# Low parts of float32 weights made by adding loads, and the lower-bound factor of a gated recurrence moved to its queries: one encoder layer on one core

## The chip, the core and the metric

The kernel runs on one core of a Trainium2 chip. The metric is the device time of one execution in microseconds; three runs of the kernel before took 849.96 to 850.8, with a median of 850.76. The engines are TensorE (PE; its weight loads are PEld), VectorE (DVE), ScalarE (ACT), GpSimd (POOL) and SyncE (SP), which here issues loads.

## The reference, cut to what matters

One layer of a hybrid encoder over 512 tokens of width 1024: token mixing (an attention group beside a bidirectional gated recurrence with 4 heads of 128), cross-attention into 256 memory tokens, and a gated MLP with a short convolution; all in float32. The gates of the recurrence are

```
f = lb_dir + (1.0 - lb_dir) * jax.nn.sigmoid(z)     # one lower bound lb per key column and direction
ks = -jnp.expm1(jnp.log(f))                         # the keys: 1 - f = (1 - lb) * sigmoid(-z)
a = jnp.einsum("...tk,...sk,...tsk->...ts", qx, kx, dec)   # query * key * decay, dec from sums of log f
...
x = x + rmsnorm(mixed, post_mix_g[l])
```

A query and a key meet only in products over the key column k, so a factor that belongs to a column and a direction can stand on either side of that product.

## The kernel before, in words

**Weights.** All weights are packed into 132 units of 128x1024 float32 (512 KB each), in the order of their use: units 0 to 3 are the recurrence's values, 4 to 6 the head 0 (query, forward gate, backward gate), 7 to 10 the output gate, 11 to 16 heads 1 and 2, 17 to 22 the attention's projections, 23 to 25 head 3, 26 to 37 keys and half the values of the memory, 38 to 41 the first half of the output projection; 42 to 131 the rest. Every product is made of three float32r matmuls (`mm3`, L134 to L137): high by high, high by low, low by high. `load_w` (L108) lets SyncE load a unit into one of two `raw` buffers; `issue` (L114) then makes its two parts with `split` (L101): ScalarE casts the unit to float32r (`wh`), and VectorE, for units 28 to 41 GpSimd (`POOL_UNITS`), subtracts that from the unit (`wl`). `wh` and `wl` have 4 buffers each. `unit` (L128) hands a unit to TensorE and issues up to three units ahead of it (`AHEAD`). Units 0 to 3 are split apart from this, by halves (L340 to L366).

**Gated recurrence.** `hgrn_in` (L449) projects a head's queries and its two gates. For each direction, `put_f` makes f and the key from z: two sigmoids on ScalarE (L462, L463), then on VectorE f times (1 - lb) plus lb (L464), the key times (1 - lb) (L465), and q times f into the query of the other direction (L466). `oml` is 1 - lb. `hgrn_core` (L476) then runs a head: the sum of the two keys (L486), its product with q (L489), and nine levels of 1 to 256 tokens, each with a copy of the keys on ScalarE (L496), matmuls (L499), two multiplications by the gates on VectorE (L525), a product of gates (L530) and a masked copy (L531).

**Around them.** `mem_norm` (L629) loads the gains and the two blocks of the memory on GpSimd's queue, squares them on ScalarE (L188), forms the roots on GpSimd (`rstd_of`, L152 to L154) and scales the rows on VectorE (L170). GpSimd has these roots, those of the heads and norms, a product with the output norm's gain (L445) and the loads of gains.

**Order.** Each engine works through its own list in order; the lists come from a scheduler that goes by the program's order and by modelled times of readiness. `weave` (L56) interleaves generators by their given weights: mixing projections beside cores 0 to 2; then core 3, the attention and the memory's projections. Cross-attention and the MLP follow.

Of the kernel before, what the change touches and what calls it, by code (L numbers as in the profile page):

```python
# [9 lines left out]
F32 = mybir.dt.float32  # L10
# [3 lines left out]
ACT = mybir.ActivationFunctionType  # L14
ALU = mybir.AluOpType
# [14 lines left out]
AHEAD = 3  # L30
HOLD_BLOCK = 4
TURN_STEP, MEM_TURN, UP_TURN = 0, (0, 4), (0, 2)
POOL_UNITS = frozenset(range(28, 42))
CORE_SHARE = 53.0
WARM = 4
LEVELS = (1, 2, 4, 8, 16, 32, 64)
# [36 lines left out]
def layer(tc, io, out):  # L73
    nc = tc.nc
# [11 lines left out]
    def small():  # L86
        return sm.tile([P, 16], F32, name="small", tag="small")

    def bank(tag):
        return ps.tile([P, 512], F32, name="ps_" + tag, tag=tag)  # L90

    def big(shape, dt=F32):
        return b8.tile(shape, dt, name="big", tag="big")

    def tmp2(shape=(P, 512), dt=F32, tag="ta"):
        return t2.tile(list(shape), dt, name="tmp2", tag=tag, bufs=TMP_BUFS[tag])
# [4 lines left out]
    def split(hi, lo, src, eng=None):  # L101
        nc.scalar.copy(hi, src)  # L102
        (eng or nc.vector).tensor_sub(lo, src, hi.bitcast(F32))  # L103

    pending, last_pow = deque(), [None]
    issued, taken, last_load = [0], [0], [None]

    def load_w():  # L108
        raw = rawp.tile([P, 1024], F32, name="raw", tag="raw")
        last_load[0] = nc.sync.dma_start(raw, io["w"][issued[0]]).ins  # L110
        issued[0] += 1
        return raw

    def issue():  # L114
        pool_unit = issued[0] in POOL_UNITS
        raw = load_w()
        wh = wp.tile([P, 1024], F32R, name="wh", tag="wh")
        wl = wp.tile([P, 1024], F32R, name="wl", tag="wl")
        split(wh, wl, raw, nc.gpsimd if pool_unit else None)
        pending.append((wh, wl))  # L120

    hold = [N_UNITS]
# [1 line left out]
    def issue_ahead():  # L124
        while issued[0] < min(hold[0], taken[0] + AHEAD):
            issue()

    def unit(n):  # L128
        taken[0] += 1
        issue_ahead()  # L130
        wh, wl = pending.popleft()
        return wh.rearrange("p (k n) -> p k n", k=n), wl.rearrange("p (k n) -> p k n", k=n)
# [6 lines left out]
    def blk(b):  # L139
        return slice(b * P, (b + 1) * P)  # L140
# [96 lines left out]
    def proj_fm(act, n, tag, use):  # L237
        o = bank(tag)
        w = unit(8)
        for kc in range(8):  # L240
            mm3(o[:, :n], (w[0][:, kc, :], w[1][:, kc, :]), act.get(kc, slice(0, n)), kc == 0, kc == 7)
            if kc % 2 and kc < 7:
                yield 6 * MM * n / 512
        use(o)
        yield 6 * MM * n / 512
# [57 lines left out]
    nhalf = const.tile([P, 16], F32, name="nhalf")  # L303
# [3 lines left out]
    nc.gpsimd.memset(ones, 1.0)  # L307
    nc.vector.memset(warm[:, :256], 0.0)
    nc.gpsimd.memset(nhalf, -0.5)

    def load_xt(kc, n):
        nc.sync.dma_start(xt[kc // 4][:, kc % 4:kc % 4 + n, :], io["xt"][:, kc:kc + n, :])

    raw = rawp.tile([P, 1024], F32, name="raw", tag="raw")
# [38 lines left out]
    for j in range(4):  # L353
        if j >= 2:
            w_raw.append(load_w())
        wh = wp.tile([P, 1024], F32R, name="wh", tag="wh")
        wl = wp.tile([P, 1024], F32R, name="wl", tag="wl")
# [15 lines left out]
    for _ in range(2):  # L373
        issue()
# [35 lines left out]
    lb = const.tile([P, 2, 4], F32, name="lb")  # L410
    oml = const.tile([P, 2, 4], F32, name="oml")
# [20 lines left out]
    def scaled(put):  # L432
        def use(o):
            z = tmp2()
            nc.vector.tensor_mul(z, o, r_bc)
            put(z)
        return use
# [11 lines left out]
    def hgrn_in(h, between=(), raw=False):  # L449
        qk = big([P, 2, 2, T])  # L450
        tt = big([P, 2048])
        q = tmp2(tag="tq")

        def put_q(z):
            nc.scalar.activation(q, z, ACT.Sigmoid)
            nc.vector.tensor_mul(q, z, q)

        def put_f(d):
            def put(z):
                f = tt[:, d * T:(d + 1) * T]  # L460
                k = qk[:, 1, d, :]
                nc.scalar.activation(f, z, ACT.Sigmoid)  # L462
                nc.scalar.activation(k, z, ACT.Sigmoid, scale=-1.0)  # L463
                nc.vector.tensor_scalar(f, f, oml[:, d, h:h + 1], lb[:, d, h:h + 1], op0=ALU.mult, op1=ALU.add)  # L464
                nc.vector.tensor_scalar(k, k, oml[:, d, h:h + 1], None, op0=ALU.mult)  # L465
                nc.vector.tensor_mul(qk[:, 0, 1 - d, :], q, f)  # L466
            return put

        for put in (put_q, put_f(0), put_f(1)):
            yield from proj_fm(raw_act if raw else hT, T, "b", scaled(put) if raw else put)  # L470
            for job in between[:2]:
                job()
            between = between[2:]
        heads[h] = (q, qk, tt)

    def hgrn_core(h):  # L476
        while h not in heads:
            yield None
        q, qk, tt = heads[h]
# [3 lines left out]
        st = room[:, 1536:1792].rearrange("p (g n) -> p g n", g=2)  # L483
        diag = a[:, :, 0, :]
        ksum = tmp2(tag="th")
        nc.vector.tensor_add(ksum, qk[:, 1, 0, :], qk[:, 1, 1, :])  # L486
        o = bank("c").rearrange("p (b n) -> p b n", b=NB)
        for b in range(NB):
            nc.tensor.matmul(o[:, b, :], ksum[:, blk(b)], q[:, blk(b)], start=True, stop=True)  # L489
# [58 lines left out]
        for b in range(NB):  # L548
            nc.vector.scalar_tensor_tensor(out=on[:, b, :], in0=o[:, b, :], scalar=r[:, b:b + 1],
                                           in1=sg_box[0][:, b, blk(h)], op0=ALU.mult, op1=ALU.mult)  # L550
# [104 lines left out]
    def cores():  # L655
        for h in range(3):
            yield from hgrn_core(h)
# [95 lines left out]
    def attention_filler():  # L753
# [7 lines left out]
        kv["y0"] = yield from res_first(mix, MIX_ORDER, lambda j: rec_done[0] == 4 if j >= 2 else att_done[0] >= 2 * j + 2)  # L761

    weave((hgrn_core(3), 22.0), (attention(), 42.0), (attention_filler(), 52.0))

    x = load_x()
# [126 lines left out]
    for kc in range(NF):  # L892
# [3 lines left out]
        w = unit(1)  # L896
# [110 lines left out]
```

## Time and profile before

| | |
|---|---|
| median of 3 runs | 850.76 us (849.96 to 850.8) |
| profiled execution, its own time | 851.05 us |
| its span, first to last instruction | 849.3 us, so 1.75 us lie around it |
| mean granted TensorE clock | 0.996 |
| busy TensorE, VectorE, ScalarE, GpSimd | 828.8, 526.6, 401.1, 95.9 us |
| loads issued by SyncE | 131 units of 512 KB and others, 77.44 MB on its queue |

Times in views of the profile are microseconds from the first instruction, unless marked ns. A row of a group gives line, engine, operation, what it writes and reads, the shape and the count, then the busy time and the mean of one, then the idle time of the engine before them. A matmul's end is modelled, so that matmuls overlap in the records; the distance from one start to the next is the pace. Times of GpSimd are rough. The chain is followed back from the last instruction to what released each step.

### The profile page before, as it was taken

The numbers are of one execution on the slowest core, as the hardware profiler recorded it, in microseconds if no ns is written. First come the engines' busy times: TensorE is split into PE (matmuls) and PEld (weight loads), VectorE is DVE, ScalarE is ACT, GpSimd is POOL, SyncE is SP. The second block draws the span as 40 slices with busy tenths as digits, with TensorE's granted clock in tenths as the row PEclk, the third lists the DMA queues.
The fourth block names the chain that finished last, engine by engine and source line by source line (L and its number), as shares of the span: only waits on it lengthen the run. The fifth ranks groups of instructions, "written<-read, shape, count | busy, mean of one in ns | idle before, by whom it ended". The sixth has DMA issues, their size and how long they took to land.

```text
span 849.3 us, 11048 instructions
## 1 busy us (share of the span) xinstructions
PE 828.8 (98%) x4304; PEld 702.9 (83%) x4304; DVE 526.6 (62%) x799; ACT 401.1 (47%) x710; POOL 95.9 (11%) x128
## 2 busy tenths in 40 slices
PE   8979999999999999999999999999999999999996
PEld 6868888887889888888888998888888888888885
DVE  5598497969997774854443865555555557722224
ACT  6563345445878884644543643333333335511121
POOL 0311100224243301300001300000000000000001
PEclk9999999999999999999999999999999999999999
DMA  9722202122222224252312242223233332322212
GB/s 323 232 76 75 74 25 87 51 76 75 75 75 91 78 81 175 75 174 75 100 50 75 76 135 98 95 94 100 100 100 99 100 100 79 101 96 97 100 49 100
DMA packets 24756, 83.52 MB, mean 98 GB/s; under 512 B 3264, under 2 KB 3904, under 8 KB 24704
## 3 DMA queue, kind: packets, MB, share of 16 engines
q1 hardware_dynamic: 22752, 77.44, 27.5%
q0 software_dynamic: 1232, 4.46, 1.7%
q10 hardware_dynamic: 720, 0.92, 0.3%
q8 instruction: 34, 0.56, 0.3%
q14 instruction: 18, 0.15, 0.1%
HBM read 80.71 MB, written 2.10 MB: 98 GB/s over the span
## 4 chain that ended last, share of the span: by engine, by line
PE 87%; DVE 6%; DMA 3%; ACT 2%; issue 1%; POOL 0%; POOLq 0%; DVEq 0%; ACTq 0%
PE ps_b L135 9%; PE ps_b L136 9%; PE ps_b L137 9%; PE ps_s L137 6%; PE ps_s L135 6%; PE ps_s L136 6%; PE ps_o L135 6%; PE ps_o L137 6%; PE ps_o L136 6%; PE ps_c L135 4%; PE ps_c L136 4%; PE ps_c L137 4%; PE ps_c L499 3%; DMA raw<-in_w_dram 2%; PE ps_o L717 2%; DVE big L525 1%
## 5 line engine op out<-in xcount | busy, mean ns | idle before, releaser
L103 DVE TENSOR_TENSOR wl<-raw,wh 128x1024 fp32r<-128x1024 f32 x114 | 139.4, 1223 | 219.7 <-ACT wh L102 219.6
L102 ACT CAST wh<-raw 128x1024 fp32r<-128x1024 f32 x128 | 134.6, 1052 | 243.5 <-PE ps_o L137 80.5
L135 PE MATMUL ps_b<-big,wh 128*128 128x512 f32 (+1 forms) x320 | 118.0, 369 | 0.0
L136 PE MATMUL ps_b<-big,wh 128*128 128x512 f32 (+1 forms) x320 | 116.6, 364 | 0.0
L137 PE MATMUL ps_b<-big,wl 128*128 128x512 f32 (+1 forms) x320 | 116.5, 364 | 0.0
L137 PEld LDWEIGHTS ps_b<-big,wl 128*128 128x128 f32 x320 | 60.3, 188 | 9.3
L135 PEld LDWEIGHTS ps_b<-big,wh 128*128 128x128 f32 x320 | 60.4, 189 | 9.1
L136 PEld LDWEIGHTS ps_b<-big,wh 128*128 128x128 f32 x320 | 60.4, 189 | 8.9
L163 POOL TENSOR_SCALAR small<-small 128x1 f32<-128x1 f32 x40 | 14.0, 350 | 440.6 <-ACT tmp L194 421.7
L135 PE MATMUL ps_s<-wh,big 128*128 128x512 f32 (+1 forms) x140 | 53.8, 384 | 0.0
L137 PE MATMUL ps_s<-wh,big 128*128 128x512 f32 (+1 forms) x140 | 53.4, 382 | 0.0
L136 PE MATMUL ps_s<-wl,big 128*128 128x512 f32 (+1 forms) x140 | 52.9, 378 | 0.0
L525 DVE TENSOR_TENSOR big<-big 128x512 f32<-128x512 f32 x64 | 49.8, 786 | 2.7 <-PE ps_c L499 1.6
L135 PE MATMUL ps_o<-wh,big 128*128 128x512 f32 (+1 forms) x124 | 47.5, 383 | 0.0
L137 PE MATMUL ps_o<-wh,big 128*128 128x512 f32 (+1 forms) x124 | 47.3, 381 | 0.0
L136 PE MATMUL ps_o<-wl,big 128*128 128x512 f32 (+1 forms) x124 | 47.1, 380 | 0.0
L103 DVE TENSOR_TENSOR big<-ps_o,big 128x512 fp32r<-128x512 f32 x52 | 35.8, 688 | 15.9 <-ACT big L102 15.5
L103 POOL TENSOR_TENSOR wl<-raw,wh 128x1024 fp32r<-128x1024 f32 x14 | 33.9, 2424 | 57.9 <-ACT wh L102 49.2
L102 ACT CAST big<-ps_o 128x512 fp32r<-128x512 f32 x52 | 30.4, 585 | 19.9 <-PE ps_o L814 7.5
L135 PE MATMUL ps_b<-wh,big 128*128 128x512 f32 x92 | 36.6, 398 | 0.0
L136 PE MATMUL ps_b<-wl,big 128*128 128x512 f32 x92 | 36.1, 392 | 0.0
L137 PE MATMUL ps_b<-wh,big 128*128 128x512 f32 x92 | 36.0, 391 | 0.0
(246 smaller groups left out, 1891.7 us busy)
## 6 DMA issues: line engine op xcount, KB each, us to landing
raw<-in_w_dram SPq DMA_DIRECT2D x131, 512.0 KB, 3.3
big<-in_x_dram SPq DMA_DIRECT2D x8, 512.0 KB, 7.3
big<-in_xt_dram SPq DMA_DIRECT2D x3, 512.0 KB, 8.0
big<-in_mem_dram POOLq DMA_DIRECT2D x2, 512.0 KB, 9.4
out_dram<-big SPq DMA_DIRECT2D x4, 256.0 KB, 2.1
out_dram<-big ACTq DMA_DIRECT2D x3, 256.0 KB, 2.1
big<-in_xt_dram SPq DMA_DIRECT2D x2, 256.0 KB, 3.4
raw<-in_w_dram SPq DMA_DIRECT2D x2, 256.0 KB, 4.0
```

Of the source, the lines that this page charges most:

```text
L102: nc.scalar.copy(hi, src)
L103: (eng or nc.vector).tensor_sub(lo, src, hi.bitcast(F32))
L135: nc.tensor.matmul(o, a[0], b[0], start=start, stop=False)
L136: nc.tensor.matmul(o, a[0], b[1], start=False, stop=False)
L137: nc.tensor.matmul(o, a[1], b[0], start=False, stop=stop)
L163: nc.gpsimd.tensor_scalar(ss[:, i + 4:i + 5], ss[:, i:i + 1], 1.0 / D, ss[:, i + 3:i + 4] if i else EPS, op0=ALU.mult, op1=ALU.add)
L499: nc.tensor.matmul(o[:, b, :], kc[:, blk(b)], pat(qk, b * P, [[2 * m, P // (2 * m)], [T + m, 2], [1, m]]), start=True, stop=True)
L525: nc.vector.tensor_tensor(out=c, in0=c, in1=pat(tt, toff + off, [[2, npair], [gap, 2], [0, m]]), op=ALU.mult)
L717: nc.tensor.matmul(o, vv[:, c, h // 4].rearrange("p a d -> p (a d)"), pt[:, j, c, :], start=c + j == 0, stop=c == 3 and j == 1)
```

## The change

`issue` makes the low part of units 4 to 41 in another way. After the cast to `wh`, `wl` is set to minus `wh`, by ScalarE for units 4 to 27 and by GpSimd for units 28 to 41, and a load issued by GpSimd reads the unit from memory a second time and adds it to `wl`. In `put_f`, f is made by ScalarE (Identity with scale and bias), the key stays without its factor (1 - lb), and the factor goes into the product of q and f. The keys' sum in `hgrn_core` takes the factors itself: half of it on ScalarE, the other half and the sum on VectorE. At the start, ScalarE copies a small tile.

```
-POOL_UNITS = frozenset(range(28, 42))
+NEG_SCALAR = frozenset(range(4, 28))
+NEG_POOL = frozenset(range(28, 42))
...
     def issue():
-        pool_unit = issued[0] in POOL_UNITS
+        i = issued[0]
         raw = load_w()
         wh = wp.tile([P, 1024], F32R, name="wh", tag="wh")
         wl = wp.tile([P, 1024], F32R, name="wl", tag="wl")
-        split(wh, wl, raw, nc.gpsimd if pool_unit else None)
+        if i in NEG_SCALAR or i in NEG_POOL:
+            nc.scalar.copy(wh, raw)
+            if i in NEG_SCALAR:
+                nc.scalar.mul(wl, wh.bitcast(F32), -1.0)
+            else:
+                nc.gpsimd.tensor_scalar(wl, wh.bitcast(F32), -1.0, 0.0, op0=ALU.mult, op1=ALU.add)
+            nc.gpsimd.dma_start(wl, io["w"][i], accum_op=ALU.add)
+        else:
+            split(wh, wl, raw)
         pending.append((wh, wl))
...
     nc.gpsimd.memset(nhalf, -0.5)
+    nc.scalar.copy(small(), nhalf)
...
-                nc.vector.tensor_scalar(f, f, oml[:, d, h:h + 1], lb[:, d, h:h + 1], op0=ALU.mult, op1=ALU.add)
-                nc.vector.tensor_scalar(k, k, oml[:, d, h:h + 1], None, op0=ALU.mult)
-                nc.vector.tensor_mul(qk[:, 0, 1 - d, :], q, f)
+                nc.scalar.activation(f, f, ACT.Identity, scale=oml[:, d, h:h + 1], bias=lb[:, d, h:h + 1])
+                nc.vector.scalar_tensor_tensor(out=qk[:, 0, 1 - d, :], in0=f, scalar=oml[:, d, h:h + 1], in1=q,
+                                               op0=ALU.mult, op1=ALU.mult)
...
-        nc.vector.tensor_add(ksum, qk[:, 1, 0, :], qk[:, 1, 1, :])
+        nc.scalar.mul(ksum, qk[:, 1, 0, :], oml[:, 0, h:h + 1])
+        nc.vector.scalar_tensor_tensor(out=ksum, in0=qk[:, 1, 1, :], scalar=oml[:, 1, h:h + 1], in1=ksum,
+                                       op0=ALU.mult, op1=ALU.add)
```

## Rows read from the trace of the kernel before

**Rows 1.** The page, busy us, share of the span and instructions of each engine.

```profile
PE 828.8 (98%) x4304; PEld 702.9 (83%) x4304; DVE 526.6 (62%) x799; ACT 401.1 (47%) x710; POOL 95.9 (11%) x128
```

**Rows 2.** Stretches: length, then busy us (count) of PE, PEld, DVE, ACT, POOL; clock, DMA share, GB/s.

```profile
0.00:20.00 20.00, 17.37 (x61) 13.68 (x62) 10.82 (x18) 12.46 (x20) 0.44 (x6) 1.00 0.90 320
...
40.00:60.00 20.00, 15.56 (x69) 12.57 (x67) 16.27 (x25) 13.81 (x20) 3.17 (x4) 1.00 0.27 86
60.00:80.00 20.00, 18.83 (x108) 16.34 (x108) 18.87 (x33) 6.27 (x9) 0.00 (x0) 0.91 0.15 52
...
140.00:160.00 20.00, 19.68 (x151) 18.45 (x150) 19.55 (x42) 9.70 (x20) 2.15 (x4) 1.00 0.17 53
...
200.00:220.00 20.00, 17.36 (x113) 15.39 (x112) 18.21 (x28) 12.69 (x22) 7.20 (x4) 1.00 0.18 59
220.00:240.00 20.00, 19.37 (x150) 17.86 (x149) 19.42 (x42) 17.14 (x36) 8.21 (x4) 1.00 0.23 80
240.00:260.00 20.00, 18.56 (x147) 17.37 (x146) 18.05 (x32) 15.16 (x32) 6.78 (x4) 1.00 0.24 80
...
640.00:660.00 20.00, 20.00 (x90) 16.58 (x89) 10.37 (x12) 8.18 (x10) 0.00 (x0) 1.00 0.25 84
```

**Rows 3.** TensorE's waits: line waited for, us in total, times, longest us.

```profile
PE ps_c L489 <- DVE tmp L486: 6.7, 2, 5.6
```

**Rows 4.** Chain that ended last, 54 to 62 us: start us, us, what.

```profile
54.50 1.05 ACT tmp L188 x2
...
60.51 0.61 DVE tmp L486
```

**Rows 5.** Chain that ended last, 200 to 216 us: start us, us, what.

```profile
202.43 2.23 DVE big L464
...
210.78 1.85 DVE big L464
...
214.89 1.16 PE ps_c L489 x8
```

**Rows 6.** VectorE's groups by form: busy us, mean ns, idle before.

```profile
L103 DVE TENSOR_TENSOR wl<-raw,wh 128x1024 fp32r<-128x1024 f32 x114 | 139.4, 1223 | 219.7 <-ACT wh L102 219.6
...
L464 DVE TENSOR_SCALAR big<-big,oml,lb 128x512 f32<-128x512 f32 x8 | 7.4, 926 | 0.3 <-ACT big L462 0.3
...
L465 DVE TENSOR_SCALAR big<-big,oml 128x512 f32<-128x512 f32 x8 | 3.8, 478 | 0.0
```

**Rows 7.** GpSimd's groups by form.

```profile
L103 POOL TENSOR_TENSOR wl<-raw,wh 128x1024 fp32r<-128x1024 f32 x14 | 33.9, 2424 | 57.9 <-ACT wh L102 49.2 <-PE ps_s L695 5.2 <-DMA raw<-in_w_dram 3.4
...
L634 POOL DMA_DIRECT2D big<-in_mem_dram x2 | 1.1, 540 | 0.0
L409 POOL CAST masks<-tmp 128x896 uint8<-128x896 f32 x1 | 0.9, 929 | 1.7 <-DMA tmp<-in_masks_dram 1.7
```

**Rows 8.** ScalarE's groups by form.

```profile
L102 ACT CAST wh<-raw 128x1024 fp32r<-128x1024 f32 x128 | 134.6, 1052 | 243.5 <-PE ps_o L137 80.5 <-PE ps_b L136 69.5 <-PE ps_c L136 33.4
...
L681 ACT ACTIVATE tmp<-tmp,small 128x512 f32<-128x512 f32 x22 | 15.8, 725 | 4.6 <-DVE small L677 4.5
...
L335 ACT ACT_TABLE_LOAD x1 | 1.3, 1283 | 3.8 <-DMA big<-in_xt_dram 3.8
```

**Rows 9.** Loads by line: queue, count, KB each, median us from issue to landing.

```profile
raw<-in_w_dram SPq DMA_DIRECT2D x131, 512.0 KB, 3.3
...
big<-in_mem_dram POOLq DMA_DIRECT2D x2, 512.0 KB, 9.4
...
big<-in_mem_norm_g_dram POOLq DMA_DIRECT2D x1, 512.0 KB, 7.9
...
big<-in_post_x_g_dram POOLq DMA_DIRECT2D x1, 512.0 KB, 4.3
```

**Rows 10.** Timelines of ScalarE and TensorE, 22 to 32 us: start us, us, what.

```profile
22.39 1.03 ACT L102 CAST wh<-raw 128x1024 fp32r<-128x1024 f32 x1
...
31.12 0.39 PE L137 MATMUL ps_b<-big,wl 128*128 128x512 f32 x1
```


## The prediction, made before the changed kernel was run

> **What bounds the kernel now.** The busy line of the page comes first: TensorE is busy for 98% of the span, VectorE for 62%, ScalarE for 47%, GpSimd for 11% [rows 1]. A change to the three vector engines can therefore only pay where TensorE waits for them, so the second view is the table of 20 us stretches [rows 2]. From about 340 us on, every stretch looks like 640:660: TensorE 20.00 of 20, 90 matmuls, one each 222 ns. That part is fixed, and no unit touched by the change lies in it. What can move is idle time before it: 4.44 us in 40:60 and 1.17 in 60:80, which belong to one wait; 0.32 in 140:160; and 2.64, 0.63 and 1.44, together 4.71, in 200:260. VectorE has 18 to 19.4 of 20 us taken in those last three stretches and 19.55 in 140:160.
>
> The third view is the list of TensorE's waits: the longest, 5.6 us, is that of L489, the first matmul of core 0, for the keys' sum of L486 [rows 3]. The fourth, the chain that ended last, says why: before L486 (60.51) stand the two squares of the memory rows on ScalarE (from 54.50), GpSimd's two roots, then the scaling L170 on VectorE [rows 4]. The wait also costs after it: the granted clock of 60:80 is 0.91, that is 9% of 20 us or some 1.8 us at less than 2.4 GHz, behind a TensorE that had done nothing. In 200:216 the chain is VectorE's: L464, the gates' multiply-and-add, stands in it with 2.23 and 1.85 us, and core 3's L489 (214.89) follows [rows 5]. The mean of L464 is 926 ns against 478 for the like L465 [rows 6]; the long ones fall together with GpSimd's 2.42 us subtractions [rows 7], so one of the two engines holds the other up.
>
> **The change, part by part.** Units 4 to 27 lose a VectorE subtraction of 1.22 us each, 29.3 us in all, and gain a ScalarE multiplication of the same 128x1024, priced by the cast of that size at 1.05 us [rows 6, 8], plus a GpSimd-issued load of the unit's 512 KB that adds onto the tile. Units 28 to 41 change GpSimd's 2.42 us subtraction for a one-input multiply-add. Its price is not shown; the nearest are the cast of 896 elements at 0.93 us below and the subtraction above, and I take 1.1 by the cast, which has one input as well. Issuing a load costs GpSimd 0.54 us [rows 7].
>
> The adding load itself is nowhere in the trace. Below it is a plain 512 KB load, 3.3 us; GpSimd's own took 4.3 in a calm stretch (the gains of the second norm) and 7.9 near the start beside other loads (those of the memory's) [rows 9]. Above I put 12.7, the 9.4 of the memory rows and 3.3 for a second pass over the bytes (an estimate from these rows). I take 7.9 at the start and 4.3 later. A unit lasts 24 matmuls of 222 ns, 5.3 us, and is prepared three units ahead, 16 us. Cast, multiplication, issue and load make 1.05 + 1.05 + 0.54 + 4.3 = 6.9 us, and 15.3 at the upper end: behind the start both fit, though the latter with hardly 1 us to spare. The 38 second reads, 19.9 MB over some 300 us, add about 66 GB/s to stretches with 52 to 86, where 0:20 moved 320: hidden.
>
> (a) *Unit 4.* Its cast runs at 22.39 and TensorE's first matmul on the low part at 31.12 [rows 10]. Now 22.39 + 1.03 + 1.05 + 0.54 + 7.9 = 32.9: TensorE waits 1.8 us (0 with 4.3, 6.6 with 12.7; more if GpSimd first does the scaled identities L382 that it is busy with then). TensorE comes 1.8 us later to a wait of 5.6, so this is nothing at the end so long as L489 is let go no later than that wait allows: the cover is that wait. If (b) removed it, the 1.8 would count.
>
> (b) *The wait of L489.* VectorE loses in 40:60 four subtractions and two pairs L464/L465, but the chain there runs over ScalarE's squares. ScalarE had 13.81 of 20 us taken; it gets four multiplications (4.2), two gates' Identity and half the sum, each like the scaled copy L681 at 0.73 [rows 8]: 6.4 more, and is full. In order, what stands before the squares holds them up, and GpSimd's roots, the scaling and the sum after them. Three multiplications and two Identities all in front would be 4.6 later; with the squares ahead of the gates the sum could start some 3.9 earlier (gates' last sigmoid at 54.5, then 0.73 + 0.73 + 0.75). Nearest is that its idle time takes most of it: I take +1.0. Queued behind GpSimd's new issues are its roots; a load that waits for a late multiplication holds those too, inside the same bounds.
>
> (c) *60 to 200 us.* ScalarE has room (6.3 to 9.7 of 20), VectorE loses some 1.2 us a unit. The idle shown is 0.32 in 140:160, with VectorE all but full. Shorter waits don't show where a matmul's modelled end reaches over the next one's start (the row of 31.12 lasts 0.39 us, and 0.22 is the pace); 0.08 us of them at each of the 14 levels of cores 1 and 2 is my estimate, with the 0.32 some -1.5. Bounds: -3, and +2.1, where two multiplications stand in front of a level's key copy.
>
> (d) *200 to 260 us.* Both L464 leave the chain, 2.23 and 1.85 us, and two L465 of 0.48; the product with q stays. Less one Identity each, 0.73, on ScalarE, that is some 3.6 us off the way to 214.89, more than the 2.64 idle of 200:220; I close that, and 0.9 of the 2.07 behind, as GpSimd's holds shrink from 2.4 to 1.1: -3.5. Next late there are the casts and Identities on ScalarE. Bounds -4.7 and 0.
>
> (e) *The small copy at the start* may bring the 1.28 us table load [rows 8] ahead of the first tile. TensorE would then only come sooner to (a)'s wait: 0, at best -1.3, and 0 if a copy needs no table.
>
> Sum: 1.0 - 1.5 - 3.5 = **-4.0 us** on this execution's 851.05 (span 849.3, 1.75 around it), that is 847.05; it stands 0.29 above the median of the runs, 850.76. Forecast **847 us**.
>
> A rule of the Trainium skill speaks against the loads: the page SBUF — State Buffer, Who interferes with whom, says that GpSimd and VectorE lock each other out of a shared pair of ports, and that descriptors which GpSimd writes for a load starve meanwhile (620 ns became about 3100). L464's 2.23 us above agrees with the lock; no run here shows the starving. By it unit 4's low part would be up to 2.5 us later, the wait 4.3 and not 1.8, and the sum -1.5 if 2.5 of it were not covered.
>
> **Rivals.** *Late low parts at the start (ends slower, 0.27).* If the adding load takes much longer than a plain one, TensorE, which waited nowhere between 31.1 and 55.6 (61.17 less 5.6), waits at unit 4 for 6.6 us and loses clock as it did in 60:80, 1.8 more; the memory rows' load and roots stand behind these issues on GpSimd, so the cover at L489 slips with it. 6.6 + 1.8 + 1.0 - 5.0 = +4.4: 855 us. It decides from about 5 us of uncovered wait, where the later gains are used up; loads near 10 us do that. For it: beside other loads they took 7.9 and 9.4, about twice the calm 4.3 [rows 9]. Against: the 7.9 is one of those.
>
> *Relief spent elsewhere (same, 0.13).* ScalarE, 15 to 17 of 20 in 220:260, or the full ScalarE of (b) becomes what TensorE waits for; (b) at +3 and (d) at -1.5, with (c) at -1.5, leave 850.8. For: the gates now take three ScalarE steps. Against: units 28 to 41 put nothing more on ScalarE.
>
> *The wait at L489 shrinks as well (faster, 0.10).* With (b) at -3.9, its clock loss of 1.8 gone and (e) at -1.3, beside (c) and (d): 851.05 - 0.29 - 12.0, about 839. For: VectorE is relieved just there. Against: the squares.
>
> The forecast itself, 842 to 849.5, has 0.50. I set what a measurement of this kernel can tell from no change at 0.2%, 1.7 us. **Range 838 to 856**: it leaves out loads slower than the bound and all gains together. Faster 0.58 (forecast and last rival, less their edge), same 0.14, slower 0.28, the rivals' own with 0.01 of that edge each.
>
> **What would show it.** Right: no VectorE wl subtraction for units 4 to 41; L464 gone and core 3's wait for the keys' sum (214.89) under 0.5 us; a wait of 0 to 3 us near 31 us, for a DMA; L489 near 62 us with a shorter wait before it; 200:260 with TensorE idle near 1.2 us. Wrong: TensorE waits for wl after 60 us, landings over 10 us, a clock row under 1.00 near 30 us, ScalarE as releaser of the keys' copy, or idle in 200:260 unchanged.

## The result, and the profile of the changed kernel

The changed kernel takes **852.34 us** (median of 6 runs, 851.94 to 854.2) against 850.51 (6 runs, 847.26 to 851.27) for the kernel before: a ratio of 1.0027, with a 95% interval of 1.0014 to 1.004. It is slower, by 1.8 us between the medians, where 847 and faster was forecast; the time lies inside the range of 838 to 856. The profiled execution took 851.94 us, its span is 850.2.

The busy line of the page does not show it: VectorE has 38 us less to do than in [rows 1], ScalarE and GpSimd have 31 and 12.5 more, and TensorE is busy for 98% of the span as before.

```profile
PE 829.1 (98%) x4304; PEld 703.2 (83%) x4304; DVE 488.9 (58%) x759; ACT 431.8 (51%) x747; POOL 108.4 (13%) x166
```

The table of stretches does, read against [rows 2] (columns as there: stretch, length, busy us and count of PE, PEld, DVE, ACT, POOL, then clock, DMA share, GB/s):

```profile
0.00:20.00 20.00, 18.41 (x72) 14.62 (x73) 10.94 (x18) 12.97 (x21) 0.45 (x6) 1.00 0.89 325
20.00:40.00 20.00, 13.68 (x55) 10.93 (x54) 4.87 (x12) 15.29 (x24) 8.06 (x11) 0.83 0.89 241
40.00:60.00 20.00, 20.00 (x90) 16.52 (x88) 12.21 (x19) 13.95 (x21) 3.39 (x5) 1.00 0.78 211
60.00:80.00 20.00, 15.98 (x89) 13.46 (x87) 16.08 (x29) 11.45 (x16) 4.20 (x7) 0.91 0.66 159
...
140.00:160.00 20.00, 19.37 (x155) 18.66 (x154) 16.91 (x39) 13.54 (x26) 4.66 (x8) 1.00 0.58 129
...
200.00:220.00 20.00, 20.00 (x126) 17.20 (x124) 15.79 (x30) 15.39 (x27) 6.73 (x8) 1.00 0.72 162
220.00:240.00 20.00, 18.98 (x144) 17.68 (x144) 18.94 (x34) 16.39 (x33) 6.19 (x6) 1.00 0.69 153
240.00:260.00 20.00, 19.66 (x157) 18.64 (x157) 17.53 (x36) 16.88 (x36) 6.55 (x7) 1.00 0.77 162
```

TensorE idles 6.32 us in 20:40, where it was never idle before; nothing in 40:60 rather than 4.44; 4.02 in 60:80 rather than 1.17. In 200:260 it idles 0 + 1.02 + 0.34 = 1.36 us rather than 4.71. So the late stage gave what was forecast, and the first 80 us, where the clock fell as well (0.83 in 20:40), took more than that. The list of TensorE's waits names the three places (columns as in [rows 3]):

```profile
PE ps_b L146 <- DMA wl<-in_w_dram: 6.3, 1, 6.3
PE ps_c L501 <- DVE tmp L497: 3.0, 1, 3.0
PE ps_c L511 <- DVE big L537: 2.0, 3, 1.0
```

The first is unit 4's low part; the second is core 0's wait for the keys' sum, 5.6 us in [rows 3]; of the third, the longest, 1.0 us at core 0's second level (69.00), is new. The chain from 24 to 70 us shows what stands before each (start us, us, what):

```profile
24.12 2.32 POOL tmp L392 x4
26.45 8.64 DMA wl<-in_w_dram
35.13 0.79 PE ps_b L146
35.92 0.43 PE ps_b L144
...
53.64 0.57 POOL wl L126
54.21 10.02 DMA big<-in_mem_dram
...
66.43 1.42 DVE big L179 x2
67.84 1.03 DVE big L537
69.00 1.20 PE ps_c L511 x8
```

Unit 4's adding load stands behind GpSimd's four scaled identities (L392), is issued at 26.45 and takes 8.64 us to land. After that wait the matmuls pace at 0.43 us, against 222 ns in the calm stretches. Two stretches cut around the wait show the clock: 0.81 us of TensorE's work in 28:35, and behind it a granted clock of 0.50, the 1.2 GHz level, for 4 us, which costs about half of them, 2 us.

```profile
28.00:35.00 7.00, 0.81 (x5) 0.37 (x4) 1.70 (x3) 3.50 (x5) 2.61 (x3) 0.83 1.01 267
35.00:39.00 4.00, 3.87 (x9) 3.10 (x10) 1.88 (x3) 4.00 (x7) 0.00 (x0) 0.50 1.06 277
```

The second half of the chain is the memory rows. Before, the gains' and both rows' loads (L148, L634) stood right behind the masks' cast in GpSimd's queue, and GpSimd made the roots from 55.6 us. Now five adding loads (L126) stand ahead of the first and a sixth ahead of the second, each waiting for ScalarE's multiplication (L123). GpSimd's timeline:

```profile
48.42 0.86 POOL L126 DMA_DIRECT2D wl<-in_w_dram  x1 [8.46 <-ACT wl L123]
48.97 0.87 POOL L157 DMA_DIRECT2D big<-in_mem_norm_g_dram  x1
49.54 0.86 POOL L646 DMA_DIRECT2D big<-in_mem_dram  x1
53.64 0.88 POOL L126 DMA_DIRECT2D wl<-in_w_dram  x1 [3.24 <-ACT wl L123]
54.21 0.85 POOL L646 DMA_DIRECT2D big<-in_mem_dram  x1
```

VectorE then meets the scaling of those rows (L179) ahead of the keys' sum (L497) and again ahead of a pair product (L537) of the first level:

```profile
60.90 1.41 DVE L179 SCALAR_TENSOR_TENSOR big<-big,small 128x512 f32<-128x512 f32 x2 [3.48 <-ACT wl L123]
62.57 0.75 DVE L497 SCALAR_TENSOR_TENSOR tmp<-big,oml,tmp 128x512 f32<-128x512 f32 x1
```

### The profile page after: what moved, and what is told of

Its sections match the earlier page's. It is cut to its first block, busy times and chain, and to the rows that moved or that the text cites. A ratio compares the mean times of both kernels' runs of the same rounds, so it can differ in the third digit from the quotient of the medians.

```text
span 850.2 us, 11098 instructions
## 1 busy us (share of the span) xinstructions
PE 829.1 (98%) x4304; PEld 703.2 (83%) x4304; DVE 488.9 (58%) x759; ACT 431.8 (51%) x747; POOL 108.4 (13%) x166
## 4 chain that ended last, share of the span: by engine, by line
PE 87%; DMA 4%; DVE 4%; ACT 3%; issue 1%; POOL 1%; SPq 0%; POOLq 0%; DVEq 0%; ACTq 0%
PE ps_b L146 9%; PE ps_b L145 9%; PE ps_b L144 9%; PE ps_s L146 6%; PE ps_s L145 6%; PE ps_s L144 6%; PE ps_o L144 6%; PE ps_o L145 6%; PE ps_o L146 6%; PE ps_c L145 4%; PE ps_c L146 4%; PE ps_c L144 4%; PE ps_c L511 3%; PE ps_o L729 2%; DMA raw<-in_w_dram 1%; DVE big L537 1%
## 5 line engine op out<-in xcount | busy, mean ns | idle before, releaser
L104 DVE TENSOR_TENSOR wl<-raw,wh 128x1024 fp32r<-128x1024 f32 x90 | 110.2, 1224 | 199.5 <-ACT wh L103 199.4
L121 ACT CAST wh<-raw 128x1024 fp32r<-128x1024 f32 x38 | 39.9, 1049 | 30.7 <-PE ps_b L145 13.4
L537 DVE TENSOR_TENSOR big<-big 128x512 f32<-128x512 f32 x64 | 49.3, 777 | 8.1 <-PE ps_c L511 3.5
L126 POOL DMA_DIRECT2D wl<-in_w_dram x38 | 34.1, 897 | 107.3 <-ACT wl L123 82.1
L144 PE MATMUL ps_b<-wh,big 128*128 128x512 f32 x92 | 36.6, 398 | 0.0
```

Of the source, the lines that this page charges most:

```text
L121: nc.scalar.copy(wh, raw)
L126: nc.gpsimd.dma_start(wl, io["w"][i], accum_op=ALU.add)
L144: nc.tensor.matmul(o, a[0], b[0], start=start, stop=False)
L537: nc.vector.tensor_tensor(out=c, in0=c, in1=pat(tt, toff + off, [[2, npair], [gap, 2], [0, m]]), op=ALU.mult)
```

## The experiments

Each time is a median, given beside that of the kernel before from runs on the same chip in between; the ratio of the runs (not quite that of the medians) and its 95% interval follow. From set to set the kernel before moved between 850.36 and 850.87, so times of different sets compare to about 0.5 us. "A" is the theory that the loss sits at the start (unit 4's late low part and the memory rows queued behind adding loads).

Two things bear on all of them. First, the busy rows understate what TensorE loses, since a matmul's modelled end reaches over the next one's start. The table counts the 4304 matmuls of each profiled execution by their starts instead, at their middle distances (0.227 us for 512 columns, 0.120 for 256, 0.111 for 128), and gives how far TensorE falls behind that pace in each stretch, in us. It is an estimate; its sums differ as the spans do, to 0.4 us. In the first column, executions of like lists differ by up to 1.8 (experiments 3, 11 and 12).

| kernel | 0:80 | 80:200 | 200:260 | 260:340 |
|---|---|---|---|---|
| before | 15.2 | 4.4 | 6.6 | 1.0 |
| changed | 20.0 | 4.2 | 3.0 | 1.0 |
| 1, new gates, no loads | 12.6 | 3.3 | 11.1 | 1.1 |
| 2, loads, old gates | 19.4 | 3.8 | 1.0 | 1.0 |
| 3, copy alone | 12.8 | 4.3 | 6.6 | 1.0 |
| 4, from unit 10, new gates | 13.5 | 3.9 | 3.3 | 1.0 |
| 5, from unit 28, new gates | 13.6 | 3.3 | 3.4 | 1.0 |
| 6, from unit 10, old gates | 12.4 | 3.6 | 1.2 | 1.0 |
| 11, from unit 28, old gates | 14.2 | 4.3 | 1.6 | 1.0 |
| 12, as 11 without loads | 14.6 | 4.5 | 1.6 | 1.0 |
| 13, all on ScalarE, new gates | 13.4 | 4.0 | 2.4 | 2.9 |
| 14, all on ScalarE, old gates | 12.1 | 3.6 | 2.5 | 2.4 |

Second, the scheduler makes every version's lists anew, and an edit can move steps that it does not name. TensorE's order is that of the kernel before in 3, 11 and 12, that of the changed kernel in 8, 9 and 10, and another in the rest. On VectorE the scaling of the memory rows stands ahead of core 0's keys' sum in the kernel before and in 3, 7, 11 and 12 (both blocks) and in the changed kernel and 8, 9 and 10 (one block); in 1, 2, 4, 5, 6, 13 and 14 it stands behind. What those experiments say of the first 80 us holds for edit and list together.

**1. New gates and copy, no adding loads.**

```diff
-NEG_SCALAR = frozenset(range(4, 28))
-NEG_POOL = frozenset(range(28, 42))
+NEG_SCALAR = frozenset()
+NEG_POOL = frozenset()
+POOL_UNITS = frozenset(range(28, 42))
...
-            split(wh, wl, raw)
+            split(wh, wl, raw, nc.gpsimd if i in POOL_UNITS else None)
```

> The new gates, the new keys' sum and the small copy stay; all low parts of weights are formed as in the kernel before (VectorE, GpSimd for units 28 to 41). Theory A (the loss sits at the start: unit 4's low part, 6.5 us of wait and some 2 of half clock, and the memory rows that queue behind the adding loads): 845 to 848 us, since the 3.4 us of idle closed in 200:260 stay and the start is that of before or a little earlier. Theory B (the three ScalarE steps of the gates cost what the loads gave): 850 or more. The first matmul on unit 4's low part waits for nothing under both.

Measured: **852.71** against 850.59, 1.0016 (1.0008 to 1.0025). A's number failed and B's was met; B's reason is weighed at 13 and 14. The start is as A had it: 73.45 of the first 80 us busy, against 71.77 in the kernel before and 68.06 in the changed one. But 200:260 got worse, with 7.30 us idle (60 − 52.70) and a lower clock:

```profile
200.00:260.00 60.00, 52.70 (x384) 47.91 (x383) 53.30 (x91) 43.73 (x84) 18.44 (x9) 0.97 0.22 71
```

So taking L464 away does not close that stage. The timelines of VectorE and GpSimd show what stands there now: a pair product (L538) meets GpSimd's subtraction (L105) and takes 3.35 us; the one before it, with GpSimd idle, took 1.15. Others beside that step took 2.9 and 2.55, and L601 2.78 rather than 0.68; VectorE's reductions from PSUM (L686) kept 0.67 to 0.69 beside it.

```profile
215.93 1.15 DVE L538 TENSOR_TENSOR big<-big 128x512 f32<-128x512 f32 x1 [0.28 <-ACT tmp L509]
217.57 3.35 DVE L538 TENSOR_TENSOR big<-big 128x512 f32<-128x512 f32 x1 [0.50 <-PE ps_c L512]
```

```profile
217.53 2.39 POOL L105 TENSOR_TENSOR wl<-raw,wh 128x1024 fp32r<-128x1024 f32 x1 [6.79 <-PE ps_c L512]
```

**2. Adding loads alone**, with the old gates and sum and without the copy.

```diff
-    nc.scalar.copy(small(), nhalf)
...
-                nc.scalar.activation(f, f, ACT.Identity, scale=oml[:, d, h:h + 1], bias=lb[:, d, h:h + 1])
-                nc.vector.scalar_tensor_tensor(out=qk[:, 0, 1 - d, :], in0=f, scalar=oml[:, d, h:h + 1], in1=q,
-                                               op0=ALU.mult, op1=ALU.mult)
+                nc.vector.tensor_scalar(f, f, oml[:, d, h:h + 1], lb[:, d, h:h + 1], op0=ALU.mult, op1=ALU.add)
+                nc.vector.tensor_scalar(k, k, oml[:, d, h:h + 1], None, op0=ALU.mult)
+                nc.vector.tensor_mul(qk[:, 0, 1 - d, :], q, f)
...
-        nc.scalar.mul(ksum, qk[:, 1, 0, :], oml[:, 0, h:h + 1])
-        nc.vector.scalar_tensor_tensor(out=ksum, in0=qk[:, 1, 1, :], scalar=oml[:, 1, h:h + 1], in1=ksum,
-                                       op0=ALU.mult, op1=ALU.add)
+        nc.vector.tensor_add(ksum, qk[:, 1, 0, :], qk[:, 1, 1, :])
```

> The adding loads for units 4 to 41 alone, on the kernel before (old gates, old sum, no small copy). Theory A: 854 to 857 us: unit 4's wait of 4 to 6.5 us with a clock row under 1.00 behind it, the wait for the keys' sum not shorter than 3 us, and nothing given back in 200:260 but what GpSimd's shorter step gives to L464 (0 to 2). Theory B: 849 to 851, as the loads relieve VectorE.

Measured: **849.0** against 850.59, 0.9977 (0.9968 to 0.9987); A's number failed, B's was met at its lower edge, and it is faster than the whole change. The start costs what A had (19.4 against 15.2 in the table; unit 4 waits 3.7 us), but the loads alone close 200:260 to 0.33 us of idle, more than they do beside the new gates (1.36):

```profile
200.00:260.00 60.00, 59.67 (x441) 55.38 (x440) 53.13 (x107) 48.39 (x92) 20.89 (x21) 1.00 0.75 167
```

**3. The small copy alone** (all else of the kernel before).

```diff
+    nc.scalar.copy(small(), nhalf)
```

> The small copy at the start alone, on the kernel before. Theory A: the first v matmul comes about 1 us earlier, and the wait for core 0's keys' sum (5.6 us before) grows by as much, since the memory rows do not come earlier: 850 to 851 us. Theory C (what is won at the start stays to the end): 848.5 to 849.5.

Measured: 850.2 against 850.59, 0.9995 (0.9983 to 1.0007): not to be told from no change. The timelines show what it does: the table load runs at 1.17 us rather than at 3.81, and the first v matmul starts at 5.17 rather than 6.38. The profiled execution, at 848.67 the second fastest of 11 (848.34 to 851.18), keeps its gain to the end: 2.4 us less lost by 80 us in the table, and the same behind. The median shows 0.4; what takes the gain in the other executions no trace shows. A's reason does not appear: the wait for the keys' sum is 5.1 us and has not grown.

**4. Adding loads from unit 10 on**; units 4 to 9 keep VectorE's subtraction.

```diff
-NEG_SCALAR = frozenset(range(4, 28))
+NEG_SCALAR = frozenset(range(10, 28))
```

> The changed kernel, but units 4 to 9 keep VectorE's subtraction; adding loads begin with unit 10, so that none stands ahead of the memory rows in GpSimd's queue. Theory A: 843 to 848 us, no wait for a load of wl before 60 us, the memory rows' loads issued near 30 us as before, 200:260 with 1.4 us idle. Theory D (adding loads cost wherever they are, by the engines that serve the loads): 850 or more, with PE idle or short waits in 80:200 where the 32 loads are.

Measured: **845.51** against 850.59, 0.9929 (0.9916 to 0.9941). A holds, D falls: the 32 loads that are left cost nothing that shows (3.9 us lost in 80:200, against 4.3 in experiment 3). With the first six the changed kernel is 6.8 us slower than this one. The idle of 200:260 is 1.37, as in the changed kernel.

```profile
200.00:260.00 60.00, 58.63 (x434) 54.15 (x434) 51.49 (x100) 50.02 (x98) 18.55 (x19) 1.00 0.72 160
```

The rows' loads are issued at 31.09 and 31.63, but no row stands ahead of the sum any more: VectorE's list has the scaling behind it.

```profile
53.89 0.75 DVE L497 SCALAR_TENSOR_TENSOR tmp<-big,oml,tmp 128x512 f32<-128x512 f32 x1 [1.26 <-ACT big L473]
...
56.69 1.42 DVE L179 SCALAR_TENSOR_TENSOR big<-big,small 128x512 f32<-128x512 f32 x2 [0.74 <-POOL small L163]
```

**5. Adding loads for units 28 to 41 alone**, new gates and copy.

```diff
-NEG_SCALAR = frozenset(range(4, 28))
+NEG_SCALAR = frozenset()
```

> New gates, sum and copy, and adding loads for units 28 to 41 alone; units 4 to 27 are split by VectorE. Theory E (the idle of 200:260 hangs on GpSimd's 2.4 us subtractions, which stretch whatever VectorE does beside them; L464 was only one victim): against 852.7 us of the run with the gates and no loads, some 6 less: 845.5 to 848, with TensorE idle under 2.5 us in 200:260 and VectorE's pair products there back from 1.23 us to 0.9 or less. Theory F (what closes 200:260 is that VectorE is rid of the splits of units 4 to 27 before): 851 to 853 with the idle of 7.3 still there.

Measured: **845.18** against 850.63, 0.9928 (0.9916 to 0.9941). E holds, 0.3 us under its range: with the splits of units 4 to 27 back on VectorE, the idle of 200:260 is 60 − 58.31 = 1.69 us, against 7.30 in experiment 1. What closes that stage is GpSimd's step.

```profile
200.00:260.00 60.00, 58.31 (x438) 53.98 (x437) 52.89 (x103) 50.49 (x99) 18.23 (x19) 1.00 0.72 159
```

**6. As 4, with the old gates and sum** (edit of 4, and that of 2 without its first line).

> Adding loads from unit 10 to 41 and the small copy, with the gates and the keys' sum of the kernel before. Theory E with the gates as a cost of their own (1.0 us of idle in 200:260, wait for ScalarE's Identity): 843 to 845 us, under the 845.5 of the same with the new gates; idle under 0.6 us in 200:260. Theory G (the new gates gain once the loads have freed ScalarE's rival, VectorE): 847 or more.

Measured: **842.38** against 850.63, 0.9901 (0.9887 to 0.9914): the fastest here, 0.6 us under E's range, 8.25 us under the kernel before and 10 under the changed one. The idle of 200:260 is 0.32.

```profile
200.00:260.00 60.00, 59.68 (x451) 55.94 (x450) 51.74 (x107) 50.23 (x98) 19.05 (x19) 1.00 0.75 168
```

**7. Memory rows' loads ahead in the queue.**

```diff
+    kv = {}
+    kv["g"], = gains("mem_norm_g")
+    kv["rows"] = big([P, MB, D])
+    for b in range(MB):
+        nc.gpsimd.dma_start(kv["rows"][:, b, :], io["mem"][blk(b), :])
     def normalize(kc):
...
     def mem_norm():
-        g_mem, = gains("mem_norm_g")
-        kv["rows"] = big([P, MB, D])
+        g_mem = kv["g"]
         for b in range(MB):
             m = kv["rows"][:, b, :]
-            nc.gpsimd.dma_start(m, io["mem"][blk(b), :])
```

> The changed kernel, but the loads of the memory's rows and gains are put ahead, behind unit 5's adding load in GpSimd's queue rather than behind unit 9's. If the memory rows' lateness is the half of the start's loss that is not unit 4's: unit 4's wait of about 6.3 us stays, the waits of 3.0 for the keys' sum and 1.0 at core 0's first level go, 847.5 to 849.5 us. If the sum is held by ScalarE's steps for the gates: 851.5 to 853.

Measured: **847.54** against 850.63, 0.9963 (0.9949 to 0.9977). The loads are issued from 28.8 us; unit 4's wait stays (5.3), the wait for the sum all but goes (0.6), as the first expectation had it:

```profile
PE ps_b L146 <- DMA wl<-in_w_dram: 5.3, 1, 5.3
PE ps_c L516 <- DVE big L542: 1.4, 3, 0.6
```

**8. Units 4 and 5 by VectorE**, memory rows still behind adding loads.

```diff
-NEG_SCALAR = frozenset(range(4, 28))
+NEG_SCALAR = frozenset(range(6, 28))
```

> The changed kernel, but units 4 and 5 keep VectorE's subtraction; the memory rows' loads still stand behind the adding loads of units 6 to 9. If unit 4's late low part costs at the end: the wait near 30 us and its half clock go (8.7 us), the wait for the keys' sum grows, but to no more than 6 us: 845 to 848 us. If the two losses cover one another (the sum comes at 62.6 us whatever TensorE did before): the wait for the sum grows to 10 us or more and the time stays at 851 to 853.

Measured: **847.58** against 850.63, 0.9964 (0.9951 to 0.9978). The time is in the first range. The profiled execution, the slowest of five (849.59), is the reverse of 7: no wait for unit 4, and one of 8.4 us for the sum, between the 6 and the 10 of the two expectations.

```profile
PE ps_c L501 <- DVE tmp L497: 8.4, 1, 8.4
```

Against experiment 4, which has neither delay (nor the loads of units 6 to 9), unit 4's late low part with early rows costs 2.0 us (847.54) and the late memory rows without it 2.1 (847.58); together they cost 6.8 (852.34). One reason is in the traces of this kernel and the changed one, whose order on TensorE is the same: here the rows' loads are issued at 45.92 and 50.59, there at 49.54 and 54.21, and core 0's first matmul on the sum starts at 60.98 here, at 63.37 there. A late unit 4 makes the later multiplications late, these the rows' loads, and these the sum, and the 2.4 us stay to the end. By the medians it is 4.8; that difference is not explained, nor how much of experiment 4's lead its list has.

**9. Plain loads for adding ones** (the addition is left out).

```diff
-            nc.gpsimd.dma_start(wl, io["w"][i], accum_op=ALU.add)
+            nc.gpsimd.dma_start(wl, io["w"][i])
```

> The changed kernel with the 38 loads of low parts as plain loads: the addition is left out, so the low part is the weight itself; every wait and issue stays. If the second pass over the bytes is the price (the page gives the adding queue's packets about twice the engine time of the others for each byte): the queue's share of the 16 engines falls from 15.4% to 8 to 10%, unit 4's landing from 8.6 us to 5 to 6.5, its wait from 6.3 to 3 to 4.5, and with it the time to 850 or 851 us; the median landing of later units falls from 5.5 to about 4. If place in the queue and the crowd of other loads make the price: share and time hardly change, 852.

Measured: 850.43 against 850.36, 0.9995 (0.998 to 1.001), about 1.9 under the changed kernel, though its ten runs spread from 846.64 to 853.8. Unit 4's load takes 6.60 us (27.46 to 34.06) and its wait falls to 4.8, so the first expectation holds but for 0.1 and 0.3 us in these two. The page's queue line and GpSimd's group of issues (busy us, mean ns), first of the changed kernel, then of this one:

```profile
q0 software_dynamic: 6704, 24.38, 15.4%
...
L126 POOL DMA_DIRECT2D wl<-in_w_dram x38 | 34.1, 897 | 107.3 <-ACT wl L123 82.1 <-ACT big L530 11.8 <-PE ps_c L511 8.1
```

```profile
q0 software_dynamic: 6704, 24.38, 9.4%
...
L126 POOL DMA_DIRECT2D wl<-in_w_dram x38 | 21.9, 577 | 112.4 <-ACT wl L123 86.5 <-ACT big L530 12.2 <-PE ps_c L511 8.4
```

Less the 1.7% that this queue had in the kernel before, the 38 loads took 13.7% of the engines' span adding and 7.7% plain: 1.8 times the engine time for the same bytes, and 0.90 rather than 0.58 us of GpSimd for each issue. So the second pass is a price, but in these two executions 2.0 of unit 4's 8.64 us; the rest a plain load has as well, in that crowd.

**10. The scaled identities on VectorE**, out of the way of unit 4's load.

```diff
-        nc.gpsimd.tensor_scalar(diag_r[:, b, :], ident, r[:, b:b + 1], None, op0=ALU.mult)
+        nc.vector.tensor_scalar(diag_r[:, b, :], ident, r[:, b:b + 1], None, op0=ALU.mult)
```

> The changed kernel with the scaled identities on VectorE, so that unit 4's adding load no longer stands behind GpSimd's four of them. If the queue ahead of it is what makes it late: issued near 25 us rather than 26.45, wait 4.8 to 5.3 us rather than 6.3, time 850.5 to 852. If it is the landing: the wait stays at 6.3, or shrinks and the wait for the keys' sum grows by as much: 852.

Measured: 852.41 against 850.36, 1.0026 (1.0014 to 1.0037). Inconclusive on the queue: in the profiled execution ScalarE waited 0.84 us for a row of x, its multiplication ended at 26.1, and the load was issued no earlier, at 26.42. It took 9.8 us, and TensorE waited longer, 7.3 us, to 36.30. Loads issued at nearly the same moment, 26.39 to 26.47, landed after 7.5 (experiment 7), 8.6, 8.7 (experiment 2) and 9.8 us: the landing, beside the x rows and the next units, is what varies.

**11. Adding loads for units 28 to 41, old gates and sum, with the copy** (edits of 5 and 6).

> Adding loads for units 28 to 41 alone, with the small copy and the old gates and sum. Theory E (only GpSimd's two-input step in 200:260 mattered): 842 to 843.5 us, the same as with loads from unit 10. If VectorE's relief in units 10 to 27 is worth something: 844 to 846, with TensorE idle 0.5 to 1 us more in 80:200.

Measured: **845.7** against 850.36, 0.9942 (0.993 to 0.9954). Above E's numbers by 2 us and in the other range. Against experiment 6 (842.38) the table puts 1.8 us in the first 80, 0.7 in 80:200 and 0.4 in 200:260. How much of that is VectorE's relief in units 10 to 27 is not shown, since the lists differ: this kernel's has both rows' scaling ahead of the sum (58.64), that of 6 has the sum first (54.28).

```profile
200.00:260.00 60.00, 59.41 (x446) 55.50 (x445) 53.83 (x110) 50.25 (x98) 19.63 (x20) 1.00 0.72 159
```

**12. The same without the loads**: GpSimd's one-input step alone.

```diff
-            nc.gpsimd.dma_start(wl, io["w"][i], accum_op=ALU.add)
```

> As the run before it, but without the adding loads of units 28 to 41: GpSimd's one-input step alone, so the addition is left out and the low part is the negated high part. Theory E, loads hidden: the same time as with them, within 1 us, idle in 200:260 under 0.6 us. If the loads are themselves a cost (engines' time, GpSimd's 0.9 us issues): 1.5 us or more faster than with them.

Measured: 845.3 against 850.36, 0.9944 (0.9932 to 0.9956), the same as with them. There the adding loads are hidden, and the whole gain is the shorter step. This is the cleanest pair here: TensorE, VectorE and ScalarE have the same instructions in the same order as in experiment 3 (850.2 us), and only GpSimd's 14 steps differ, 2.42 us each there and 1.08 here.

```profile
200.00:260.00 60.00, 59.43 (x446) 55.52 (x445) 53.90 (x110) 49.94 (x97) 11.29 (x11) 1.00 0.24 80
```

**13 and 14. The negated high parts of units 28 to 41 on ScalarE too**, loads from unit 10 on; 13 with the new gates, 14 with the old.

```diff
-NEG_SCALAR = frozenset(range(4, 28))
-NEG_POOL = frozenset(range(28, 42))
+NEG_SCALAR = frozenset(range(10, 42))
+NEG_POOL = frozenset()
```

> New gates, sum and copy; adding loads from unit 10 to 41, and ScalarE makes the negated high part for all of them, also for units 28 to 41, so that GpSimd only issues loads there. Theory E (a VectorE step that falls together with GpSimd's step is stretched; the gates only shift which): the wait of 1.06 us for the second head's transposes goes, no pair product over 1.3 us, idle in 200:260 under 0.7 us, 843.5 to 845 against 845.5. Theory H (ScalarE's own steps are the cost of the gates): ScalarE gets 1.05 us more a unit in a stretch where it had 17 of 20 taken, idle in 200:260 of 2 us or more, 846 or more.

> The same with the old gates and sum. Theory E: GpSimd's stretch is gone for every VectorE step, idle in 200:260 near that of 842.4's run (0.3 us), 841.5 to 843. Theory H: as good as with the multiplications on GpSimd, or up to 1 us worse; the gap to the run with the new gates is 3 us or more.

Measured: **846.68** (0.9952, 0.9938 to 0.9966) and **845.1** (0.9935, 0.9922 to 0.9948) against 850.87. In time both lie above E's numbers; in the busy rows of 200:260 they do as E said. First 13, then 14:

```profile
200.00:260.00 60.00, 59.71 (x438) 55.07 (x437) 49.90 (x101) 57.29 (x107) 7.79 (x9) 1.00 0.71 159
260.00:280.00 20.00, 19.35 (x125) 16.93 (x124) 10.35 (x23) 17.44 (x39) 3.81 (x5) 1.00 0.71 160
280.00:300.00 20.00, 19.73 (x114) 16.09 (x113) 15.26 (x32) 17.52 (x37) 1.79 (x2) 1.00 0.51 118
```

```profile
200.00:260.00 60.00, 59.49 (x443) 55.34 (x442) 50.80 (x105) 56.40 (x105) 8.15 (x10) 1.00 0.72 164
```

The idle of 200:260 is 0.29 with the new gates and 0.51 with the old, and no pair product there takes over 1.17 us. By the table 2.4 and 2.5 us are lost there, so the rows hide some 2 us in both, but the new gates cost nothing beside the old: with GpSimd out of the way their price is gone, and the three ScalarE steps of theories B and H are not it. What is left is ScalarE itself, with 57 and 56 of 60 us taken: it runs late in 260:300 too, where TensorE loses 2.9 and 2.4 us rather than the 1.0 of experiment 4. That is H's bottleneck, with either pair of gates.

Put together, with the new gates and with the old TensorE idles in 200:260 for 7.30 and 4.70 us beside GpSimd's subtraction (experiments 1 and 3), 1.37 and 0.32 beside its one-input step (4 and 6), 0.29 and 0.51 with neither (13 and 14). By the table the new gates cost 4.5 us there beside the subtraction, 2.1 beside the step, and nothing with neither.

## Why the prediction was wrong

**Terms (a) and (b), the first 80 us: +1.0 forecast, +4.8 measured** (20.0 less 15.2 in the table; by the medians +6.8 against experiment 4, which takes both delays away, and has another list and not the relief of units 4 to 9). This is the step that failed, and it failed in its cover: the first 80 us make 3.8 of the 4.9 us by which the profiled span misses the forecast's −4.0.

- *(a)* I had unit 4's low part ready at 32.9 and TensorE there at 31.12, so 1.8 us of wait. It was ready at about 35.1: the cast was 0.36 later than in [rows 10], the load was issued 1.56 us after the multiplication (24.89), because L392 stood in the queue, which I mentioned in a bracket and did not count; the landing took 8.64, not 7.9. TensorE came earlier, at about 28.8, with the small copy's help (without it, in experiment 2, at about 31.5). The wait of 6.3 is close to the upper end of my bound, 6.6, though not by the slower load that I put there. The half clock behind it, some 2 us, I had priced in the rival and not in the term.
- The cover was to be the wait of 5.6 at L489. It did shrink, to 3.0, but the sum itself slipped, from 60.51 [rows 4] to 62.57, and with it core 0's first matmul from 61.17 to 63.37; a further 1.0 came at L511. I wrote that GpSimd's roots queue behind its new issues "inside the same bounds" and did not follow the memory rows' *loads*: they went from about 30 us to 49.54 and 54.21. Experiments 7 and 8 show it: with the rows early the cover takes all but 2 us of (a), the late rows without (a) cost 2 as well, and both at once 6.8. The trace of 8 shows that (a) itself moves what ends the cover: without it the rows' loads go out 3.6 us earlier and core 0 starts 2.4 us earlier.

The first rival had this mechanism: a wait of 6.6, 1.8 of clock, the cover slipping as the memory rows queue on GpSimd, 855 us. It got 0.27. The sign of the forecast hung on that choice.

**Terms (c), (d) and (e): −5.0 forecast.** Experiment 4 stands 5.1 under its kernel before, but that agrees by luck: by the table 1.7 of it lie in the first 80 us, 0.5 in 80:200 and 3.3 in 200:260.

- *(c)* was forecast at −1.5 and gave next to nothing: 4.2 us lost in 80:200 of the changed kernel, 4.4 before. This is the rest of the miss. The new gates with VectorE's splits have 3.3 there (experiments 1 and 5, against 4.3 in 3 and 11).
- *(e)* brought the table load ahead, as said, and no time clear of noise (experiment 3).
- *(d)* came to 4.71 − 1.36 = −3.35 of idle (−3.6 in the table) against −3.5, yet **by another cause**. I put 2.64 of it on L464 leaving the chain and 0.9 on GpSimd's shorter holds; experiment 1 took L464 away and the idle rose to 7.30. The gain is GpSimd's two-input subtraction of 2.42 us [rows 7] becoming a step of 1.10 (experiments 5 and 12). L464's 2.23 us was the price of meeting that subtraction, and the new gates let L538, L601 and the sum meet it instead. Beside the one-input step they still cost 2.1 us there, and 1.1 in the first 80 us and 0.3 in 80:200, which make up the gap between experiments 4 and 6 (3.1 us in the medians, 3.4 in the spans). With the loads on units 28 to 41 alone they cost as much there (3.4 against 1.6, experiments 5 and 11) and have it back before (845.18 and 845.7).

A slip that changes nothing: the 3.9 of (b) is 3.8 by its own numbers (60.51 less 56.71).

On this the Trainium skill was nearer than I was: the page SBUF — State Buffer, section Who interferes with whom, says that a VectorE instruction with two inputs in SBUF contends with a GpSimd instruction that reads SBUF. L538 has two such inputs, and its 3.35 us beside GpSimd's 2.39 agrees. The starving of GpSimd's descriptors, which I had set against the loads (that page of the Trainium skill has its figure in the section A bandwidth-pool intuition that's wrong), does not show in the issues: in the first 80 us of the changed kernel each issue of an adding load took GpSimd 0.86 to 1.03 us. Whether some of the landings' 7.5 to 9.8 us is starving, no run separates.

## What to carry to other kernels

When work moves onto a queue, list every instruction already in that queue behind the new ones, loads first, and ask when each will now be issued; a load that waits for another engine's result holds up all loads behind it. A cover only counts if what ends it is not itself moved by the change. And when an instruction is slow because another engine is in its way, removing it can pass the slowness on to the next one that meets that engine: shorten the other engine's step. A version compared with another has its own lists too; look at what else moved. The version to keep here is experiment 6: adding loads from unit 10 on, GpSimd's one-input step, the old gates, 842.38 us.

## What the hardware showed that I had not expected

- An adding load takes 1.8 times the DMA engines' time of a plain one for the same bytes (13.7% against 7.7% of the span), and its issue 0.90 us of GpSimd against 0.58. The plain loads of the memory rows, in the same queue, were also dearer to issue beside them: 0.85 us each, against 0.54 before and in experiment 9. Yet the 32 adding loads from 53 us on in experiment 4 cost no time that shows.
- GpSimd's step can lengthen a 128x512 pair product beside it by nearly its own length: 1.15 to 3.35 us by a step of 2.39 (experiment 1), 1.16 to 2.04 by one of 1.05 (experiment 4). Reductions from PSUM beside the same steps kept 0.66 to 0.69 us.
- A 6.3 us wait, early in the kernel, was followed by 4 us at the 1.2 GHz level.
